# Gate and up of three feed-forwards by Strassen's seven block products, with the modulation sums spread over three engines

## The chip, the core and the metric

The kernel runs on one core of a Trainium2 chip. It uses all five engines: TensorE (PE in the profile) for matrix products, with its weight loads as PEld; VectorE (DVE); ScalarE (ACT); GpSimd (POOL); and SyncE (SP), which issues the DMAs. The metric is the device time of one execution in microseconds.

## The reference

Two layers of a diffusion backbone over 256 latent and 256 context tokens, with a model dimension of 1024. Each layer is a feed-forward, token mixing (attention), and a second feed-forward; each of the three reads a norm that is modulated by vectors computed from the conditioning. All is float32.

```python
def rms_norm(x): return x * rsqrt(mean(x * x, axis=-1) + EPS)
def modulate(h, shift, scale): return h * (1.0 + scale) + shift
def swiglu(h, w_gate, w_up, w_down): return (silu(h @ w_gate) * (h @ w_up)) @ w_down

# layer l: nine vectors of 1024 for the latent tokens (from c), nine for the context tokens (from c_ctx)
m = silu(c) @ w_mod[l] + b_mod[l]            # w_mod[l]: 1024 x 9216
x = x + 0.5 * m[2] * swiglu(modulate(rms_norm(x), m[0], m[1]), ffn1_w_gate[l], ffn1_w_up[l], ffn1_w_down[l])
x = x + m[5] * mix(modulate(rms_norm(x), m[3], m[4]))
x = x + 0.5 * m[8] * swiglu(modulate(rms_norm(x), m[6], m[7]), ffn2_w_gate[l], ffn2_w_up[l], ffn2_w_down[l])
```

The gate and up weights are 1024 x 2816, the down weights 2816 x 1024. The output is the latent stream after two layers, so that the context tokens aren't needed after the second layer's mixing: three feed-forwards have 512 tokens (numbered 1 to 3 below), the last one 256.

## The kernel before

Activations lie transposed: a tile has 128 channels on the partitions and the tokens as columns, the 256 latent tokens first (`HALF[0]`), then the 256 context tokens (`HALF[1]`). Weights are the stationary operand.

**Products in three parts.** A float32 operand is held as a high part (ScalarE copies it to the type that TensorE reads, `fp32r`) and a low part (VectorE subtracts the high part from the operand); `split`, L99, does both. `mm3`, L106, issues three products: high by high, high by low, low by high. `wcols`, L290, loads a block of weights (4 chunks of 128 rows by 256 columns, 512 KB) into a `raw` tile and splits it into an `hs` tile. There are 3 `raw` and 5 `hs` buffers.

**Feed-forward.** `ffn`, L406, goes over 22 chunks of 128 inner columns in pairs, `pair`, L410: gate and up, for each 2 chunks x 8 chunks of the contraction x 3 parts = 48 products of 128 x 128 weights with 512 columns, gathered in PSUM banks `gps` and `ups`; then Silu, product, and a split of the result into an `ah` tile. The 11 pairs come in two parts (`FFN_PARTS`, 6 and 5 pairs). After each part the down products of its chunks (`down`, L477; PSUM `dps`) are added to the stream `xT` by VectorE (`residual`, L313), scaled by the modulation vector. In the last part the second half of the down products is done for each token half apart, so that the next norm can start.

**Modulation.** Except for the first two vectors, the 16 others are sums over the 1024 rows of `w_mod` that run beside the feed-forwards: `mod_load` brings two blocks of 128 x 512, `mod_part`, L198, multiplies each with one scalar a partition and adds it to an accumulator `macc`, once for the latent and once for the context conditioning, all on VectorE. `mod_end`, L209, sums over the partitions with TensorE. `pump_every`, L282, takes one such turn (two blocks) for each 512 columns of products issued, until the list of vectors is done; lists are queued for each feed-forward (six vectors for 1, four for 2, six for 3).

**Order.** The program is written in this order; a scheduler then sets the order of each engine's queue. Queues run in order. SP issues all DMAs.

## Time and profile before

| | us |
|---|---|
| median of 3 executions | 1836.57 |
| lowest, highest | 1834.9, 1838.31 |
| profiled execution, its own time | 1838.31 |
| its span, first to last instruction | 1838.3 |
| TensorE busy in it | 1790.1 |
| VectorE busy | 1278.7 |
| ScalarE busy | 732.8 |
| GpSimd busy | 45.5 |

The times of the profile come from one execution, of the length of the slowest of the three. Busy time is the time in which an engine has an instruction in work; instructions overlap at their edges, so a group's busy time can be less than its count by the mean duration. On TensorE only busy time by count, or the length of a run of products in the chain, tells the pace of products; the mean duration of one holds its way through the array as well. A line in the profile can be that of a helper: L101 is the subtraction in `split`, L104 the product in `mm`, L94 and L97 are `mul` and `add`.

### The profile page before, as it was taken

What the parts mean: (1) busy time and instruction counts of PE and PEld (TensorE: products, weight loads), DVE (VectorE), ACT (ScalarE), POOL (GpSimd) and SP (SyncE); (2) the same over time, 40 slices, a digit from 0 to 9 for tenths busy, and PEclk for the clock granted to TensorE, in tenths of its full rate; (3) what the DMA queues carried; (4) which work ended last, traced back from release to release, by engine and by line L of the source; (5) the groups of instructions that cost most, each with busy time, mean ns of one, the idle gap of its engine ahead of it and who ended that gap; (6) DMA issues with size and microseconds to landing.
All of it is one profiled execution on the core that took longest, in us unless ns stands there. A gap on an engine that the chain in (4) does not pass through costs nothing.

```text
span 1838.3 us, 27533 instructions
## 1 busy us (share of the span) xinstructions
PE 1790.1 (97%) x10851; PEld 1549.1 (84%) x10851; DVE 1278.7 (70%) x2458; ACT 732.8 (40%) x1316; POOL 45.5 (2%) x25
## 2 busy tenths in 40 slices
PE   7999999999999989999999999999999988999999
PEld 4788888898998888888888988888889987789998
DVE  5998776457788699877434667777336787877564
ACT  4323122335666553221223333212234656664442
POOL 0000000011010000000000000000001011000000
PEclk9999999999999989999999999999999999999999
DMA  9856564322110246656323245564333542146552
GB/s 301 271 192 195 191 195 135 117 60 79 49 59 19 65 130 214 207 191 207 116 92 104 77 128 193 186 210 146 91 115 87 101 99 57 47 150 206 172 184 81
DMA packets 229549, 253.80 MB, mean 138 GB/s; under 512 B 21388, under 2 KB 195628, under 8 KB 229420
## 3 DMA queue, kind: packets, MB, share of 16 engines
q1 hardware_dynamic: 229420, 252.05, 44.4%
q8 instruction: 85, 1.39, 0.3%
q14 instruction: 44, 0.36, 0.1%
HBM read 250.96 MB, written 1.05 MB: 137 GB/s over the span
## 4 chain that ended last, share of the span: by engine, by line
PE 85%; DVE 7%; ACT 3%; DMA 2%; issue 1%; SPq 1%; DVEq 0%; ACTq 0%
PE ups L104 23%; PE gps L104 23%; PE dps L104 23%; PE ops L104 3%; PE po L781 2%; PE sc L104 2%; DMA bias<-in_d_rpb_dram 1%; DVE hs L101 1%; PE mps L213 1%; PE paq L104 1%; PE trp L684 1%; PE pbk L104 1%; PE pbv L104 1%; PE bpo L104 1%; PE pak L104 1%
## 5 line engine op out<-in xcount | busy, mean ns | idle before, releaser
L100 ACT ACTIVATE hs<-raw 128x1024 fp32r<-128x1024 f32 (+2 forms) x308 | 315.4, 1030 | 611.9 <-PE dps L104 195.3
L101 DVE TENSOR_TENSOR hs<-raw,hs 128x1024 fp32r<-128x1024 f32 (+2 forms) x308 | 366.9, 1196 | 228.3 <-ACT hs L100 226.2
L104 PE MATMUL dps<-ah,hs 128*128 128x512 f32 (+1 forms) x2256 | 403.5, 338 | 0.2 <-DVE hs L101 0.2
L104 PEld LDWEIGHTS dps<-ah,hs 128*128 128x128 f32 x2256 | 349.8, 190 | 47.7 <-issue 2.5
L104 PE MATMUL gps<-hT,hs 128*128 128x512 f32 (+1 forms) x1680 | 377.8, 381 | 3.8 <-ACT hT L567 2.7
L104 PE MATMUL ups<-hT,hs 128*128 128x512 f32 (+1 forms) x1680 | 374.9, 379 | 0.0
L104 PEld LDWEIGHTS gps<-hT,hs 128*128 128x128 f32 x1680 | 304.1, 190 | 66.0 <-ACT hT L567 3.5
L104 PEld LDWEIGHTS ups<-hT,hs 128*128 128x128 f32 x1680 | 303.2, 189 | 60.3 <-issue 2.4
L206 DVE SCALAR_TENSOR_TENSOR macc<-mraw,const,macc 128x512 f32<-128x512 f32 x448 | 308.7, 745 | 2.7 <-DMA mraw<-in_w_mod_dram 2.5
L320 DVE SCALAR_TENSOR_TENSOR xT<-dps,const,xT 128x256 f32<-128x256 f32 x112 | 50.2, 478 | 78.4 <-PE dps L104 78.3
L100 ACT ACTIVATE ah<-af 128x512 fp32r<-128x512 f32 (+1 forms) x88 | 50.3, 572 | 99.5 <-DVE af L94 68.1
L301 POOL TENSOR_TENSOR hs<-raw,hs 128x1024 fp32r<-128x1024 f32 (+2 forms) x21 | 45.3, 2160 | 1582.8 <-ACT hs L300 1505.9
L104 PE MATMUL gps<-hTl,hs 128*128 128x258 f32 x528 | 66.8, 284 | 1.6 <-DVE hTl L398 1.0
L104 PEld LDWEIGHTS gps<-hTl,hs 128*128 128x128 f32 x528 | 64.7, 190 | 2.5 <-DVE hTl L398 1.2
L104 PE MATMUL ups<-hTl,hs 128*128 128x258 f32 x528 | 65.5, 283 | 0.0
L104 PEld LDWEIGHTS ups<-hTl,hs 128*128 128x128 f32 x528 | 64.4, 190 | 0.0
L101 DVE TENSOR_TENSOR ah<-af,ah 128x512 fp32r<-128x512 f32 (+1 forms) x88 | 54.4, 619 | 13.4 <-ACT ah L100 13.1
L453 ACT ACTIVATE sg<-gps 128x512 f32<-128x512 f32 x66 | 38.3, 588 | 57.9 <-PE gps L104 57.9
L94 DVE TENSOR_TENSOR af<-sg,ups 128x512 f32<-128x512 f32 x66 | 45.1, 685 | 22.5 <-PE ups L104 22.1
L709 DVE TENSOR_REDUCE nm<-sc 128x1 f32<-128x512 f32 (+1 forms) x80 | 53.7, 681 | 5.9 <-PE sc L104 5.8
L715 ACT ACTIVATE pr<-sc,nm 128x512 f32<-128x512 f32 (+1 forms) x64 | 40.3, 635 | 14.9 <-DVE nm L709 14.2
L329 ACT ACTIVATE sq<-xT 128x256 f32<-128x256 f32 (+1 forms) x54 | 23.5, 448 | 51.0 <-DVE xT L320 50.8
(303 smaller groups left out, 1950.0 us busy)
## 6 DMA issues: line engine op xcount, KB each, us to landing
mraw<-in_w_mod_dram SPq DMA_DIRECT2D x128, 512.0 KB, 4.7
raw<-in_ffn_w_gate_dram SPq DMA_DIRECT2D x88, 512.0 KB, 4.1
raw<-in_ffn_w_up_dram SPq DMA_DIRECT2D x88, 512.0 KB, 4.4
raw<-in_ffn_w_down_dram SPq DMA_DIRECT2D x80, 512.0 KB, 3.4
raw<-in_cd_w_in_dram SPq DMA_DIRECT2D x18, 512.0 KB, 4.0
wm<-in_w_mod_dram SPq DMA_DIRECT2D x16, 512.0 KB, 8.6
raw<-in_ab_w_in_dram SPq DMA_DIRECT2D x16, 512.0 KB, 4.1
raw<-in_ffn_w_down_dram SPq DMA_DIRECT2D x16, 256.0 KB, 2.7
```

Source lines behind the costliest of these rows:

```text
L94: V.tensor_tensor(out=out_, in0=a, in1=b, op=ALU.mult)
L100: S.activation(h, src, AF.Copy)
L101: V.tensor_tensor(out=l, in0=src, in1=h.bitcast(F32), op=ALU.subtract)
L104: T.matmul(ps, a, b, start=start, stop=stop)
L206: V.scalar_tensor_tensor(out=acc[:, v], in0=raw[:, i], scalar=c, in1=acc[:, v], op0=ALU.mult, op1=ALU.add)
L301: nc.gpsimd.tensor_tensor(out=hs[:, 1, :n], in0=raw[:, :n], in1=hs[:, 0, :n].bitcast(F32), op=ALU.subtract)
L320: V.scalar_tensor_tensor(out=xT[dc][:, a:e], in0=ps[:, a:e], scalar=modT[:, l, v, m, dc:dc + 1], in1=xT[dc][:, a:e], op0=ALU.mult, op1=ALU ...
L329: S.activation(sq[:, cols], xT[dc][:, cols], AF.Square)
L453: S.activation(sg, g[:, :ntok], AF.Silu)
L709: V.tensor_reduce(out=nm[:, c], in_=view, axis=AX.X, op=ALU.max, negate=True)
L715: S.activation(p[:, cols], sc[:, cols], AF.Exp, bias=nm[:, i + b:i + b + 1], accum_out=den[:, i + b:i + b + 1])
L781: T.matmul(po[64 * x:64 * x + 64, q], val(x, c), pts[x][c], start=c == order[0], stop=c == order[-1], tile_position=(0, 64 * x))
```

## The change

It has two parts.

**Seven products.** In feed-forwards 1 to 3 all pairs but the first (`FFN_PLAIN`) are done by `quad_pair`, which calls `quad` for gate and again for up: 60 quads in all. A quad takes the weights of a pair as 2 x 2 blocks (contraction halves by the two chunks) and the activations as 2 x 2 blocks (contraction halves by token halves), and makes the pair's result from seven block products in place of eight, each 4 chunks x 3 parts = 12 products of 256 columns, by Winograd's form of Strassen's scheme. The combined weight blocks are sums that GpSimd makes of the raw weights (`wquads`: four sums of 128 x 512), and all seven blocks are split. The combined activation blocks are made once a norm, by GpSimd (`combine`: 16 sums of 128 x 256) from unsplit copies that ScalarE keeps (`keep`). VectorE sums the block products out of PSUM (four sums a quad). Parts are now of 3, 3, 3 and 2 pairs, so that each feed-forward has four stages of down products; the last, 256-token feed-forward keeps 6 and 5 pairs and plain products.

**Modulation.** VectorE keeps the latent half. For the context half ScalarE scales the block in place and GpSimd adds it to the accumulator. The context half of four vectors of the second layer, which nothing reads, is left out.

Buffers: `hs` has 8 tiles of half the size (a quad takes seven), `raw` 5, the weights of the first two vectors (`wm`) 6 instead of 16.

```diff
-FFN_PARTS = (6, 5)
+FFN_PARTS = {(0, 1): (3, 3, 3, 2), (0, 2): (3, 3, 3, 2), (1, 1): (3, 3, 3, 2), (1, 2): (6, 5)}
+FFN_PLAIN = {(0, 1): 1, (0, 2): 1, (1, 1): 1, (1, 2): 11}
...
-    def mod_part(acc, raw, k):
+    def mod_part(acc, raw, k, both):
         for i in range(2):
-            for v in range(2):
-                c = cT[:, k + i, v:v + 1]
-                if k + i == 0:
-                    V.tensor_scalar(out=acc[:, v], in0=raw[:, i], scalar1=c, scalar2=None, op0=ALU.mult)
-                else:
-                    V.scalar_tensor_tensor(out=acc[:, v], in0=raw[:, i], scalar=c, in1=acc[:, v], op0=ALU.mult,
-                                           op1=ALU.add)
+            c = cT[:, k + i, 0:1]
+            if k + i == 0:
+                V.tensor_scalar(out=acc[:, 0], in0=raw[:, i], scalar1=c, scalar2=None, op0=ALU.mult)
+            else:
+                V.scalar_tensor_tensor(out=acc[:, 0], in0=raw[:, i], scalar=c, in1=acc[:, 0], op0=ALU.mult,
+                                       op1=ALU.add)
+        for i in range(2 if both else 0):
+            c = cT[:, k + i, 1:2]
+            if k + i == 0:
+                S.activation(acc[:, 1], raw[:, i], AF.Copy, scale=c)
+            else:
+                S.activation(raw[:, i], raw[:, i], AF.Copy, scale=c)
+                nc.gpsimd.tensor_tensor(out=acc[:, 1], in0=raw[:, i], in1=acc[:, 1], op=ALU.add)
...
+    def wquads(w, fp):
+        a = []
+        for b in range(2):
+            raw = rawp.tile([P, 1024], F32, tag="raw", name="rq")
...
+        (a11, a21), (a12, a22) = [[t[:, x] for x in range(2)] for t in a]
+        sw = [unit("sw", "sw") for _ in range(3)]
+        s3, s2, s1 = [t.rearrange("p (k f) -> p k f", f=P) for t in sw]
+        G = nc.gpsimd.tensor_tensor
...
+        parts("a12", a12)
+        parts("a11", a11)
+        G(out=s3, in0=a11, in1=a21, op=ALU.subtract)
+        G(out=s1, in0=a21, in1=a22, op=ALU.add)
+        G(out=s2, in0=s1, in1=a11, op=ALU.subtract)
+        parts("s3", s3)
+        parts("s2", s2)
+        G(out=a21, in0=a12, in1=s2, op=ALU.subtract)
+        parts("s1", s1)
+        parts("s4", a21)
+        parts("a22", a22)
...
+    def combine():
+        G = nc.gpsimd.tensor_tensor
+        for j in range(4):
+            t = hL[j]
+            for i, (a, b) in enumerate(((1, 0), (2, 1), (2, 0), (3, 2))):
+                G(out=t[:, i], in0=t[:, a], in1=t[:, b], op=ALU.subtract)
+            hC[j] = [hp.tile([P, 4, 256], R32, tag="hS", name="hC", bufs=UNITS["hS"]) for _ in range(2)]
+            split(*hC[j], t)
...
+            def prod(ps, x):
+                an, bk = b[x]
+                for k in range(4):
+                    mm3(ps, a[an][:, 0, k], a[an][:, 1, k], bk(k, 0), bk(k, 1), k == 0, k == 3)
...
+            pump_every(512)
+            x, y, z, e = [bank(tag, f"{nm}q{tag}") for tag in ("mm", "sc", "mm", "sc")]
+            prod(x[:, lat], "p2")
+            prod(e[:, lat], "p1")
+            s1 = unit("wq", f"{nm}p1")[:, lat]
+            S.activation(s1, e[:, lat], AF.Copy)
+            prod(x[:, ctx_], "p6")
+            t, r = unit("wq", f"{nm}t"), unit("wq", f"{nm}r")
+            add(two(t), two(x), both(s1))
+            prod(y[:, ctx_], "p7")
+            prod(y[:, lat], "p5")
+            add(two(r), two(y), both(t[:, ctx_]))
+            add(t[:, ctx_], y[:, lat], r[:, ctx_])
+            pump_every(512)
+            prod(z[:, ctx_], "p4")
+            prod(z[:, lat], "p3")
+            add(r, r, z)
+            return t, r
```

What it makes of the queues is shown at three places, all in feed-forward 1. TensorE, one pair in the middle of its last part before (`gps` and `ups` in two banks each):

```order
L104 MATMUL gps_2272<-hT,hs 128x512 x12
L104 MATMUL gps_2273<-hT,hs 128x512 x12
L104 MATMUL gps_2272<-hT,hs 128x512 x12
L104 MATMUL gps_2273<-hT,hs 128x512 x12
L104 MATMUL ups_2284<-hT,hs 128x512 x12
```

TensorE, gate's quad of a pair in the third part after (`hB` and `hT` are norm tiles, `hC` the combined ones, `gqmm` and `gqsc` PSUM banks):

```order
L107 MATMUL gqmm<-hT,hs 128x256 x12
L107 MATMUL gqsc<-hB,hs 128x256 x12
L107 MATMUL gqmm<-hC,hs 128x256 x12
L107 MATMUL gqsc<-hC,hs 128x256 x24
L107 MATMUL gqmm<-hC,hs 128x256 x12
L107 MATMUL gqmm<-hT,hs 128x256 x12
```

48 products of 512 columns have become 84 of 256. VectorE, around the same pair before (`hs<-raw` is a weight block's low part, `af` gate by up, `ah` its low part):

```order
L101 TENSOR_TENSOR hs<-raw,hs 128x1024
L206 SCALAR_TENSOR_TENSOR macc<-mraw,const,macc 128x512 x2
L101 TENSOR_TENSOR hs<-raw,hs 128x1024
L94 TENSOR_TENSOR af<-sg,ups_2284 128x512
L101 TENSOR_TENSOR ah<-af,ah 128x512
L94 TENSOR_TENSOR af<-sg,ups_2285 128x512
```

VectorE, a stretch of the second part after (`rq` and `sw` are raw and combined weight blocks, `gt` and `gr` the sums of products):

```order
L100 TENSOR_TENSOR gt<-gqmm,gp_2016 128x512
L208 SCALAR_TENSOR_TENSOR macc<-mraw,const,macc 128x512
L104 TENSOR_TENSOR hs<-rq,hs 128x512
L208 SCALAR_TENSOR_TENSOR macc<-mraw,const,macc 128x512
L100 TENSOR_TENSOR gr<-gqsc,gt 128x512
L104 TENSOR_TENSOR hs<-sw,hs 128x512
L100 TENSOR_TENSOR gt<-gqsc,gr 128x256
L104 TENSOR_TENSOR hs<-sw,hs 128x512 x2
L100 TENSOR_TENSOR gr<-gr,gqmm 128x512
```

Sums out of PSUM now stand between the low parts of the next quad's weights. GpSimd before, its whole work of the program (low parts of the mixing layers' weights):

```order
L301 TENSOR_TENSOR hs<-raw,hs 128x1024 x6
L301 TENSOR_TENSOR hs<-raw,hs 128x512 x2
L301 TENSOR_TENSOR hs<-raw,hs 128x1024 x7
L301 TENSOR_TENSOR hs<-raw,hs 128x768 x3
L301 TENSOR_TENSOR hs<-raw,hs 128x512 x2
L301 TENSOR_TENSOR hs<-raw,hs 128x1024
```

GpSimd after, two quads of the third part of feed-forward 1 (L344 to L349 are the four sums of `wquads`, L216 the context half of the modulation):

```order
L344 TENSOR_TENSOR sw<-rq 128x512
L216 TENSOR_TENSOR macc<-mraw,macc 128x512 x4
L345 TENSOR_TENSOR sw<-rq 128x512
L346 TENSOR_TENSOR sw<-sw,rq 128x512
L349 TENSOR_TENSOR rq<-rq,sw 128x4x128
L344 TENSOR_TENSOR sw<-rq 128x512
L216 TENSOR_TENSOR macc<-mraw,macc 128x512 x3
L345 TENSOR_TENSOR sw<-rq 128x512
L346 TENSOR_TENSOR sw<-sw,rq 128x512
L349 TENSOR_TENSOR rq<-rq,sw 128x4x128
```

The feed-forwards, in which GpSimd had nothing before, now give it four sums a quad and up to four for the modulation.

## Rows read from the trace of the kernel before

**Rows 1.** The page, parts 1 and 2: span, busy time by engine, granted clock in 40 slices.

```profile
span 1838.3 us, 27533 instructions
PE 1790.1 (97%) x10851; PEld 1549.1 (84%) x10851; DVE 1278.7 (70%) x2458; ACT 732.8 (40%) x1316; POOL 45.5 (2%) x25
...
PEclk9999999999999989999999999999999999999999
```

**Rows 2.** The chain that ended last, in order of time: start, us, what (three pieces).

```profile
58.90 10.88 PE gps L104 x48
...
193.99 38.11 PE dps L104 x168
...
1709.67 34.55 PE dps L104 x288
```

**Rows 3.** Windows, all engines: feed-forward 1 with modulation running, feed-forward 2 after it.

```profile
core 0: us, PE busy (x) PEld busy (x) DVE busy (x) ACT busy (x) POOL busy (x), PEclk, DMA share, GB/s
120.00:160.00 40.00, 40.00 (x190) 32.36 (x189) 33.82 (x54) 11.89 (x16) 0.00 (x0) 1.00 0.53 177
880.00:920.00 40.00, 40.00 (x178) 33.10 (x178) 14.20 (x16) 11.89 (x15) 0.00 (x0) 1.00 0.40 120
```

**Rows 4.** Groups by line and form, VectorE and ScalarE: names, shapes, count | busy us, mean ns | idle.

```profile
L101 DVE TENSOR_TENSOR hs<-raw,hs 128x1024 fp32r<-128x1024 f32 x286 | 348.4, 1224 | 227.5 <-ACT hs L100 225.5 <-DMA bias<-in_d_rpb_dram 1.5
...
L206 DVE SCALAR_TENSOR_TENSOR macc<-mraw,const,macc 128x512 f32<-128x512 f32 x448 | 308.7, 745 | 2.7 <-DMA mraw<-in_w_mod_dram 2.5
...
L320 DVE SCALAR_TENSOR_TENSOR xT<-dps,const,xT 128x256 f32<-128x256 f32 x112 | 50.2, 478 | 78.4 <-PE dps L104 78.3
...
L101 DVE TENSOR_TENSOR ah<-af,ah 128x512 fp32r<-128x512 f32 x66 | 45.2, 687 | 13.4 <-ACT ah L100 13.1
...
L94 DVE TENSOR_TENSOR af<-sg,ups 128x512 f32<-128x512 f32 x66 | 45.1, 685 | 22.5 <-PE ups L104 22.1
...
L100 ACT ACTIVATE ah<-af 128x512 fp32r<-128x512 f32 x66 | 41.2, 625 | 68.1 <-DVE af L94 68.1
...
L453 ACT ACTIVATE sg<-gps 128x512 f32<-128x512 f32 x66 | 38.3, 588 | 57.9 <-PE gps L104 57.9
```

**Rows 5.** The page, part 6: issue of the first norm's modulation weights, count, KB, us to landing.

```profile
wm<-in_w_mod_dram SPq DMA_DIRECT2D x16, 512.0 KB, 8.6
```

**Rows 6.** Timeline from 376.3 us, GpSimd and VectorE: start us, us, engine, line, operation.

```profile
start us, us, engine line op out<-in xcount [idle before <-releaser]
...
376.56 2.41 POOL L301 TENSOR_TENSOR hs<-raw,hs 128x1024 fp32r<-128x1024 f32 x1 [376.12 <-ACT hs L300]
376.78 0.88 DVE L320 SCALAR_TENSOR_TENSOR xT<-dps,const,xT 128x256 f32<-128x256 f32 x2 [4.48 <-PE dps L104]
...
378.14 0.48 DVE L320 SCALAR_TENSOR_TENSOR xT<-dps,const,xT 128x256 f32<-128x256 f32 x1 [0.48 <-PE dps L104]
...
378.54 0.97 DVE L97 TENSOR_TENSOR const<-const,sq 128x512 f32<-128x512 f32 x1
```

**Rows 7.** Timeline from 1626 us, GpSimd and VectorE.

```profile
1626.10 2.40 POOL L301 TENSOR_TENSOR hs<-raw,hs 128x1024 fp32r<-128x1024 f32 x1 [39.03 <-PE ops L104]
...
1626.51 2.54 DVE L101 TENSOR_TENSOR hs<-raw,hs 128x512 fp32r<-128x512 f32 x1
```

**Rows 8.** Timeline from 1406.3 us, VectorE and GpSimd.

```profile
1406.33 1.21 DVE L101 TENSOR_TENSOR hs<-raw,hs 128x1024 fp32r<-128x1024 f32 x1
...
1406.97 2.84 POOL L301 TENSOR_TENSOR hs<-raw,hs 128x1024 fp32r<-128x1024 f32 x1 [8.16 <-ACT hs L300]
```

**Rows 9.** Groups by line and form, GpSimd.

```profile
L301 POOL TENSOR_TENSOR hs<-raw,hs 128x1024 fp32r<-128x1024 f32 x14 | 34.6, 2473 | 1444.2 <-ACT hs L300 1367.3 <-PE ops L104 39.0 <-DMA bias<-in_d_rpb_dram 27.9
L301 POOL TENSOR_TENSOR hs<-raw,hs 128x768 fp32r<-128x768 f32 x3 | 5.5, 1869 | 10.7 <-ACT hs L300 10.7
L301 POOL TENSOR_TENSOR hs<-raw,hs 128x512 fp32r<-128x512 f32 x4 | 5.1, 1287 | 127.9 <-ACT hs L300 127.9
```

**Rows 10.** Windows, all engines, around a drop of the granted clock (columns as above).

```profile
640.00:655.00 15.00, 12.20 (x102) 12.00 (x100) 14.52 (x35) 9.47 (x20) 0.00 (x0) 1.00 0.13 36
655.20:665.40 10.20, 7.35 (x31) 6.87 (x32) 9.75 (x27) 4.44 (x12) 0.00 (x0) 0.50 0.61 206
```

**Rows 11.** Windows, TensorE products into gps alone: busy (count), clock, DMA share, GB/s.

```profile
661.20:665.40 4.20, 4.20 (x19) 0.50 0.45 172
```

More of the change, by code (lines that the diff above doesn't have):

```diff
@@ L1 @@
 import math
-from contextlib import ExitStack
+from contextlib import ExitStack, nullcontext
 import concourse.bass as bass
@@ L293, in wcols @@
         raw = rawp.tile([P, 1024], F32, tag="raw", name="raw")
-        Q.dma_start(out=raw[:, :n].rearrange("p (k f) -> p k f", k=nk), in_=src)
+        last_load[0] = Q.dma_start(out=raw[:, :n].rearrange("p (k f) -> p k f", k=nk), in_=src).ins
         if tag is None:
-            hs = hsp.tile([P, 2, 1024], R32, tag="hs", name="hs")
+            parts = [hsp.tile([P, 1024], R32, tag="hs", name="hs")[:, :n] for _ in range(2)]
         else:
-            hs = big("hw", tag)
+            hw = big("hw", tag)
+            parts = [hw[:, s, :n] for s in range(2)]
@@ L310, in tile_hybrid_dit, with hx, new_hT @@
     hT = [None] * KC
+    def hx(k, s, sl):
+        t = hT[k]
+        if isinstance(t, tuple):
+            v = sl.start // 256
+            return t[v][:, s, sl.start - 256 * v:sl.stop - 256 * v]
+        return t[:, s, sl]
+    def new_hT(split_):
+        two = [[hp.tile([P, 2, 2, 256], R32, tag="hB", name="hB", bufs=UNITS["hB"]) for _ in range(2)]
+               for _ in range(2)] if split_ else []
+        for k in range(KC):
+            if split_ and k < 4:
+                hT[k] = tuple(t[k // 2][:, k % 2] for t in two)
+            else:
+                hT[k] = hp.tile([P, 2, NTOK], R32, tag="hT", name="hT")
     summed = set()
@@ L364, in norm_half @@
         if v == 0:
-            for k in range(KC):
-                hT[k] = hp.tile([P, 2, NTOK], R32, tag="hT", name="hT")
+            new_hT(m != 3)
         bc = norm_stats(l, m, v)
@@ new lines, in quad_pair @@
+        def quad_pair(g):
+            with tc.issue_after(last_load[0]) if g == FFN_PLAIN[l, n] else nullcontext():
+                gs = quad("g", wg, g)
+                for t in gs:
+                    S.activation(t, t, AF.Silu)
+                us = quad("u", wu, g)
+            ah = [big("ah") for _ in range(2)]
+            for i, (sg, t) in enumerate(zip(gs, us)):
+                mul(t, t, sg)
+                for s in range(2):
+                    flat = ah[s].rearrange("p i n -> p (i n)")
+                    o = flat[:, 256:768] if i else bass.AP(tensor=flat.tensor, offset=flat.offset, ap=[flat.ap[0], [768, 2], [1, 256]])
+                    if s == 0:
+                        S.activation(o, t if i else t.rearrange("p (x n) -> p x n", x=2), AF.Copy)
+                        hi = o
+                    else:
+                        V.tensor_tensor(out=o, in0=t if i else t.rearrange("p (x n) -> p x n", x=2), in1=hi.bitcast(F32), op=ALU.subtract)
+            return [[ah[s][:, i] for s in range(2)] for i in range(2)]
@@ L468, in ffn @@
         f0 = 0
-        for part, npair in enumerate(FFN_PARTS):
+        n = 1 if m_gate == 2 else 2
+        for part, npair in enumerate(FFN_PARTS[l, n]):
             acts = []
             for fp in range(npair):
-                acts += pair(f0 // 2 + fp, 2 * fp, part == 0 and fp == 0)
+                if f0 // 2 + fp < FFN_PLAIN[l, n]:
+                    acts += [[t[:, s] for s in range(2)]
+                             for t in pair(f0 // 2 + fp, 2 * fp, part == 0 and fp == 0)]
+                else:
+                    acts += quad_pair(f0 // 2 + fp)
@@ L473, in ffn @@
             nf = 2 * npair
-            last = part == 1
-            if mixing is not None and not last:
+            last = part == len(FFN_PARTS[l, n]) - 1
+            if mixing is not None and part == 0:
                 next(mixing)
@@ L587, in tile_hybrid_dit @@
         V.tensor_copy(bcs[:, HALF[v]], norm_bcast(rs0[:, 2 * v:2 * v + 2])[:, :256])
-    hT[:] = [hp.tile([P, 2, NTOK], R32, tag="hT", name="hT") for k in range(KC)]
+    new_hT(True)
     first_mods(0, wm0)
```

98 lines of the change are left out of this document (69 added, 29 removed).

## The prediction

> **What bounds the kernel now.** I began with the page's busy shares. The matrix engine (PE) is busy 1790.1 of 1838.3 us, so 48 us are left in which it isn't; VectorE (DVE) stands at 70%, GpSimd (POOL) at 2% [rows 1]. The chain of waits then shows what a feed-forward is made of: runs of nothing but products. 48 of them with 512 columns take 10.88 us (227 ns each), 168 take 38.11 us; 288 with 256 columns take 34.55 us (120 ns each) [rows 2]. A product of half the width thus costs 53%, not 50%. Inside a feed-forward the windows show PE busy 40.00 of 40 us, with DVE at 33.82 while the modulation stream runs and at 14.20 once it is done [rows 3]. So PE sets the time, and every product that goes is worth its 120 or 227 ns, as long as the other engines keep delivering weights. DVE has 6 us in 40 to spare in the first kind of stretch. That is the number to watch, since the change puts work on DVE's side in all of them.
>
> The execution profiled took 1838.31 us, its span 1838.3; the median of the three is 1836.57, 1.7 us less. A difference of 0.2% (4 us) is about what a measurement of this kernel can tell from no change.
>
> **What the change saves on PE.** A chunk pair's gate (or up) was 48 products of 512 columns, 10.88 us [rows 2]. As a "quad" it is 7 block products of 12, 84 products of 256 columns: 84 x 0.120 = 10.08 us. Each of the 60 quads saves 0.80 us, 48 us in all. Smaller shares of the down products come in halves (288 + 528 half-width ones instead of 1248: about -3 us) and half of the first pair of feed-forward 1 becomes half-width (+1 us). PE: -50 us.
>
> The Trainium skill (TensorE: Matmul & The Clock Gate, Back-to-back issue gap) gives the spacing of single products as columns / 2.4 + 2.5 ns, 109 ns at 256 and 216 ns at 512. By that a quad would save 1.2 us and the change 72 us; the rows say 120 and 227 ns, and they decide.
>
> **What it puts on the other engines.** For each quad, by the code and the order:
> - Splits of seven 512-column blocks into high and low parts instead of two of 1024: ACT seven copies, DVE seven subtractions of two SBUF tiles.
> - GpSimd four sums of 512 columns on the weights, 240 in all, plus 16 sums of 256 columns at each of three norms.
> - DVE four sums that read PSUM (2.4 us by the 0.69 us of a 512-column sum [rows 4] and half for the short one).
> - For a pair, DVE's products of gate and up and the low parts of the result, as before, but now all from SBUF: 2 a quad.
> - The modulation stream: DVE keeps the latent half (256 of 512 operations); the context half becomes a scaling on ACT and a sum on GpSimd (168), and is dropped for four of the 16 vectors.
>
> ACT carries this: 7 x 0.63 + half of two Silu and two copies, 1.2, + 0.4 + at most 2.2 for modulation = 8.2 us a quad, under 10.1 [rows 4]. The loads keep their number and size. Early loads have 6 buffers instead of 16: 0 to 8.6 us (one round of them [rows 5]); I take 3, as most of the first pair's products stand before the last quarter. The 96 more residual updates (48 for each of two more parts, 0.45 us [rows 4]) read PSUM and lie in the down stages, where DVE has room.
>
> **What decides: GpSimd and DVE exclude each other.** At 376.56 a GpSimd sum runs for 2.41 us. Three DVE updates that read PSUM pass beside it at their usual 0.48 us. Then a 512-column sum of two SBUF tiles starts at 378.54 and ends at 379.51, 0.54 us after GpSimd's end at 378.97 [rows 6]. At 1626.51 a weight split of 512 columns takes 2.54 us instead of 0.69 and ends 0.55 us after GpSimd [rows 4, 7]. The other way round too: at 1406.97 GpSimd finds DVE in a split, takes 2.84 instead of 2.41 us, and ends 2.27 us after that split [rows 8]. So of a GpSimd sum and a DVE operation with two SBUF inputs only one runs at a time, for its whole length, and their times add up. Before, GpSimd worked 45.5 us in the whole program [rows 1]; now it has 408 sums of 512 columns inside the feed-forwards, and nearly all of DVE's work there has two SBUF inputs: splits, modulation, the result's products and low parts.
>
> Prices. A DVE operation of 512 columns: 0.69 us alone, 0.55 behind a GpSimd sum; I take 0.62 (the two will alternate, but not always). Of 1024: 1.22 and, by the same 0.14 less, 1.09; I take 1.15. GpSimd's of 512: 1.29 alone [rows 9], 1.15 with the 0.14 us that the row at 1406.97 hides; I take 1.20. Of 256, an estimate from 1.29, 1.87 and 2.47 us for 512, 768 and 1024 [rows 9]: 0.65.
>
> One quad with both halves of the modulation: 13 DVE operations x 0.62 + 7.5 GpSimd sums x 1.20 = 17.1 us, against PE's 10.1. With the latent half alone: 13 x 0.62 + 4 x 1.20 = 12.9. Without modulation: 9 x 0.62 + 4.8 = 10.4. The sums that read PSUM (2.4) I take as hidden under GpSimd's time. Since PE needs the splits of each quad, and the buffers hold little more than one quad's seven blocks, it can't run ahead.
>
> Now the sum over the stretches. Each feed-forward has four blocks of products (a plain pair and 4 quads; 6; 6; 4 quads), each followed by its down products (33 us, the last 24). I counted the operations of each block in the order. The second block of feed-forward 1: DVE 36 splits, 27 modulation steps, 12 products and low parts, 2 short weight splits, 77 x 0.62 = 48, and 3 x 1.15; GpSimd 24 + 22 sums x 1.20 = 55. Together 106 us, against 60.5 of PE: +46. The others in the same way, as operations on DVE (of 512, of 1024) and GpSimd, excess over PE:
> - Feed-forward 1: first block 60, 9 and 24 (+16 short), 94 against 62, of which 10 lie in the start-up: +22. Second: +46. Third 70, 3 and 48: 104 against 60.5, +44. Fourth, no modulation, 31, 4 and 16: +3. In all +115.
> - Feed-forward 2: 67, 8 and 28 (+16 short), 5 us of it before the first product: +31. 78, 3 and 49: +50. 50, 3 and 31: +11. Fourth +2. In all +94.
> - Feed-forward 3 (latent half alone for four of six vectors): 66, 9 and 34 (+16 short), 8 us before the first product: +35. 76, 3 and 24: +19. 61, 3 and 24: +10. Fourth +2. In all +66.
>
> The down stages come out about even: in the first of feed-forward 1, DVE's 18 us and GpSimd's 17 sums, 20 us, against 33; the others have less, and I leave these 5 us to the range.
>
> Sum: 1838 - 50 + 275 + 3 = 2066, against the median 2064; I say **2065 us**, 12% slower. At the low prices (0.55, 1.09, 1.15) the 944 us of such work shrink by 8%: 1990. At the high ones (0.69, 1.22, 1.29): 2150. With none of the 2.4 us hidden in the 48 quads of the first three blocks, 115 more: 2265.
>
> **Rivals.**
> - *Faster after all.* GpSimd's sums fall into the time that DVE spends on PSUM (2.4 us a quad, and the residual updates) or waits for ACT and PE, and exclusion costs little. DVE alone then needs 13 x 0.62 + 2.4 = 10.5 us a quad, PE 10.1: about even, and the 50 us are gained: 1790. The point is where the two engines' sum passes PE's 10.1 us a quad; by the rows it is passed by 7 us while modulation runs for both halves. For it: 408 sums are only 490 us, beside some 1040 us of products (60 x 10.08, three pairs of 21.8 and three times 123 of down products). Against: DVE's two-input work there is 620 us more. 10%.
> - *The clock falls as well.* PE waits inside most quads. At 655.2 its granted clock shows 0.50 (1.2 of 2.4 GHz) for 10.2 us, after 15 us in which it was busy 12.20 [rows 10]; there 19 half-width products took 4.20 us [rows 11], 221 ns each, a quad 18.6 us. If it stayed there through the first three blocks of all three (136 us more a feed-forward than PE's full speed), the time would be 1838 - 50 + 408 = 2196. For it: PE would be busy 60% of such a block. Against: at half speed it waits no longer, and comes back. 15%. The Trainium skill (TensorE: Matmul & The Clock Gate, HAM oscillation — how this bites in real kernels) describes just this, bursts that each start at half rate behind a wait for data; the row at 655.2 agrees with it for one wait, and no row here shows it over a long stretch.
> - *Late sums.* DVE's queue is in order. A sum that reads PSUM stands between splits, and while it waits for a product the next quad's splits wait behind it, GpSimd's buffers with them. That is the 2265 above. 5%.
>
> **How the numbers follow.** The forecast itself has 68%, within no change 2%, the rivals 10, 15 and 5%. The range of 1930 to 2200 takes in both ends of the prices and the clock's case; left out are the gain, no change and the time above 2200. Faster 0.10, same 0.02, slower 0.88.
>
> **What would show it.** Right: GpSimd busy about 550 us; DVE's splits of 512 columns at well over 0.69 us on average, those beside a GpSimd sum ending 0.55 us behind it; PE's waits for DVE's splits the longest of all; blocks with both modulation halves near 17 us a quad, those at the end near 10.5. The clock's part: stretches at 0.5 in the first three blocks. Wrong: PE still above 95% busy in the feed-forwards, GpSimd's sums beside two-input DVE work without stretching it, or ACT late instead.

## The result, and the profile after

The changed kernel takes 2082.74 us (median of 4 executions, 2080.02 to 2084.0) against 1836.9 before (4 executions in the same session): a ratio of 1.1335, with a 95% interval of 1.1319 to 1.1351. The forecast was 2065, with a range of 1930 to 2200. It is 246 us slower.

The page of the kernel after, parts 1 and 2, beside [rows 1]:

```profile
span 2082.1 us, 33783 instructions
...
PE 1838.2 (88%) x12811; PEld 1672.8 (80%) x12811; DVE 1716.5 (82%) x2858; ACT 1022.6 (49%) x1940; POOL 748.7 (36%) x481
...
PEclk9898998999999988888999989999999999999999
```

GpSimd has gone from 45.5 to 748.7 us, VectorE from 1278.7 to 1716.5. PE's share fell from 97% to 88%, and its clock is no longer full in the feed-forwards. The groups by line and form show what VectorE's and GpSimd's operations now last (busy, mean ns, then idle time before them); [rows 4] and [rows 9] have the same operations before: 745 ns for a modulation step, 687 for a split of 512 columns, 1287 for a GpSimd sum:

```profile
L208 DVE SCALAR_TENSOR_TENSOR macc<-mraw,const,macc 128x512 f32<-128x512 f32 x224 | 239.1, 1068 | 24.7 <-DMA mraw<-in_w_mod_dram 23.3
L104 DVE TENSOR_TENSOR hs<-rq,hs 128x512 fp32r<-128x512 f32 x240 | 230.2, 974 | 22.5 <-ACT hs L103 22.3
L104 DVE TENSOR_TENSOR hs<-sw,hs 128x512 fp32r<-128x512 f32 x180 | 208.7, 1184 | 12.7 <-ACT hs L103 12.3
...
L216 POOL TENSOR_TENSOR macc<-mraw,macc 128x512 f32<-128x512 f32 x168 | 265.6, 1582 | 233.9 <-ACT mraw L215 181.7 <-issue 46.2 <-DVE nrm L460 1.5
L345 POOL TENSOR_TENSOR sw<-rq 128x512 f32<-128x512 f32 x60 | 97.5, 1625 | 162.5 <-DMA rq<-in_ffn_w_gate_dram 82.6 <-DMA rq<-in_ffn_w_up_dram 52.3 <-PE gqsc L107 9.0
```

The idle time ahead of VectorE's groups is short, but their operations last up to 1.7 times as long as alone. Sorted by what GpSimd did meanwhile, splits of `rq` that meet no GpSimd operation last 682 ns on average (135 of them), those that meet a sum of 512 columns 1354 (101). A record of busy time here holds waiting that no semaphore shows. The timeline of the kernel after, from 349.9 us, VectorE and GpSimd, in the third block of feed-forward 1:

```profile
349.94 1.59 POOL L346 TENSOR_TENSOR sw<-sw,rq 128x512 f32<-128x512 f32 x1
350.34 1.75 DVE L208 SCALAR_TENSOR_TENSOR macc<-mraw,const,macc 128x512 f32<-128x512 f32 x1
351.61 1.60 POOL L349 TENSOR_TENSOR rq<-rq,sw 128x512 f32<-128x512 f32 x1
352.01 1.75 DVE L104 TENSOR_TENSOR hs<-sw,hs 128x512 fp32r<-128x512 f32 x1
...
353.17 1.71 POOL L344 TENSOR_TENSOR sw<-rq 128x512 f32<-128x512 f32 x1
353.68 0.68 DVE L100 TENSOR_TENSOR ur<-uqsc,ut 128x512 f32<-128x512 f32 x1
354.28 1.15 DVE L208 SCALAR_TENSOR_TENSOR macc<-mraw,const,macc 128x512 f32<-128x512 f32 x1
```

Read the ends. GpSimd ends at 351.53, VectorE's modulation step at 352.09, 0.56 us behind; GpSimd's next at 353.21, 1.12 behind that; VectorE's split at 353.76, 0.55 behind. They take turns, 1.67 us for a pair, though each record shows 1.6 to 1.75 us for one. The sum that reads PSUM (353.68) passes beside GpSimd in 0.68 us. The Trainium skill (SBUF — State Buffer, SBUF: two separate sides) says that the two engines share a pair of SBUF ports as an exclusive lock: of a VectorE operation with two SBUF inputs and a GpSimd operation that reads SBUF, the one that starts first holds it for the whole instruction, and the other waits. The turns in these rows agree.

Windows of the kernel after, all engines (columns as in [rows 3]): in feed-forward 1 the first down stage, the second and third blocks of products, and the fourth, which has no modulation left:

```profile
135.90:185.40 49.50, 39.86 (x165) 30.33 (x163) 48.02 (x70) 19.83 (x31) 37.35 (x23) 0.86 0.47 150
185.40:271.20 85.80, 71.02 (x525) 67.48 (x524) 84.36 (x100) 46.83 (x81) 55.31 (x36) 0.92 0.44 135
...
314.60:412.00 97.40, 73.83 (x541) 69.98 (x540) 95.25 (x107) 48.23 (x83) 65.29 (x41) 0.89 0.45 134
...
444.80:485.00 40.20, 40.20 (x337) 40.20 (x336) 33.68 (x47) 22.01 (x36) 11.36 (x7) 1.00 0.45 132
```

VectorE is busy for 97 to 98% of the first three, PE for 76 to 83%; in the last, four quads take 40.20 us with PE busy throughout, 10.05 each. PE stands idle for 244 us of the span, before for 48. Of its waits (us in all, times, longest), those for the low parts of quads are the longest in total; three lines of the list:

```profile
PE gqmm L107 <- DVE hs L104: 29.0, 15, 4.4
PE nst L107 <- DVE const L100: 19.7, 5, 7.0
PE mps L227 <- POOL macc L216: 14.2, 7, 3.9
```

By stages, from the first product of one to the first of the next: feed-forward 1 takes 489 us instead of 385, 2 takes 452 instead of 372, 3 takes 412 instead of 374, and the mixing layers 266 and 240 instead of 253 and 229.

### The profile page after: what moved, and what is told of

It is laid out like the page before. It is cut to its first block, busy times and chain, and to the rows that moved or that the text cites. A ratio compares the mean times of both kernels' runs of the same rounds, so it can differ in the third digit from the quotient of the medians.

```text
span 2082.1 us, 33783 instructions
## 1 busy us (share of the span) xinstructions
PE 1838.2 (88%) x12811; PEld 1672.8 (80%) x12811; DVE 1716.5 (82%) x2858; ACT 1022.6 (49%) x1940; POOL 748.7 (36%) x481
## 4 chain that ended last, share of the span: by engine, by line
PE 27%; DVE 15%; issue 4%; DMA 3%; ACT 2%; POOL 1%; SPq 0%; DVEq 0%; ACTq 0%; POOLq 0%
PE dps L107 9%; DVE hs L104 5%; PE ups L107 3%; PE gps L107 3%; DMA mraw<-in_w_mod_dram 2%; DVE macc L208 2%; PE uqmm L107 2%; PE gqmm L107 2%; PE uqsc L107 1%; DVE xT L387 1%; PE gqsc L107 1%; DVE const L100 1%; DMA bias<-in_d_rpb_dram 1%; PE po L941 1%; POOL hL L407 1%
## 5 line engine op out<-in xcount | busy, mean ns | idle before, releaser
L216 POOL TENSOR_TENSOR macc<-mraw,macc 128x512 f32<-128x512 f32 x168 | 265.6, 1582 | 233.9 <-ACT mraw L215 181.7
L104 DVE TENSOR_TENSOR hs<-raw,hs 128x1024 fp32r<-128x1024 f32 (+3 forms) x212 | 253.0, 1201 | 56.3 <-ACT hs L103 52.1
L208 DVE SCALAR_TENSOR_TENSOR macc<-mraw,const,macc 128x512 f32<-128x512 f32 x224 | 239.1, 1068 | 24.7 <-DMA mraw<-in_w_mod_dram 23.3
L103 ACT ACTIVATE hs<-raw 128x1024 fp32r<-128x1024 f32 (+3 forms) x212 | 196.4, 941 | 109.4 <-PE dps L107 67.1
L104 DVE TENSOR_TENSOR hs<-rq,hs 128x512 fp32r<-128x512 f32 x240 | 230.2, 974 | 22.5 <-ACT hs L103 22.3
L215 ACT ACTIVATE mraw<-mraw,const 128x512 f32<-128x512 f32 x168 | 120.5, 720 | 211.6 <-DVE macc L208 180.8
L104 DVE TENSOR_TENSOR hs<-sw,hs 128x512 fp32r<-128x512 f32 x180 | 208.7, 1184 | 12.7 <-ACT hs L103 12.3
L103 ACT ACTIVATE hs<-rq 128x512 fp32r<-128x512 f32 x240 | 143.8, 620 | 76.3 <-PE dps L107 33.2
L344 POOL TENSOR_TENSOR sw<-rq 128x512 f32<-128x512 f32 x60 | 102.8, 1713 | 156.5 <-DMA rq<-in_ffn_w_gate_dram 150.0
L345 POOL TENSOR_TENSOR sw<-rq 128x512 f32<-128x512 f32 x60 | 97.5, 1625 | 162.5 <-DMA rq<-in_ffn_w_gate_dram 82.6
L107 PE MATMUL gqmm<-hC,hs 128*128 128x256 f32 x720 | 109.0, 301 | 35.6 <-DVE hs L104 25.5
L103 ACT ACTIVATE hs<-sw 128x512 fp32r<-128x512 f32 x180 | 105.4, 621 | 46.4 <-PE dps L107 23.1
L107 PE MATMUL gqmm<-hT,hs 128*128 128x256 f32 x720 | 105.5, 299 | 13.2 <-DVE ut L100 6.3
```

The source lines that it names most:

```text
L103: S.activation(h, src, AF.Copy)
L104: V.tensor_tensor(out=l, in0=src, in1=h.bitcast(F32), op=ALU.subtract)
L107: T.matmul(ps, a, b, start=start, stop=stop)
L208: V.scalar_tensor_tensor(out=acc[:, 0], in0=raw[:, i], scalar=c, in1=acc[:, 0], op0=ALU.mult, op1=ALU.add)
L215: S.activation(raw[:, i], raw[:, i], AF.Copy, scale=c)
L216: nc.gpsimd.tensor_tensor(out=acc[:, 1], in0=raw[:, i], in1=acc[:, 1], op=ALU.add)
```

## Experiments

All times are device times; the kernel before took 1835 to 1838 us beside each group. Where one number is given, it is that of one execution.

### GpSimd's sums: what they cost, and by what

**One column of the context sums.** ScalarE's scaling, the steps and their order stay; the other 511 columns of these 168 sums are left out.

```diff
-                nc.gpsimd.tensor_tensor(out=acc[:, 1], in0=raw[:, i], in1=acc[:, 1], op=ALU.add)
+                nc.gpsimd.tensor_tensor(out=acc[:, 1, 0:1], in0=raw[:, i, 0:1], in1=acc[:, 1, 0:1], op=ALU.add)
```

> The changed kernel with GpSimd's 168 sums of the context modulation cut to one column (the context modulation vectors are then wrong; DVE's and ScalarE's work is unchanged). Exclusion theory (a GpSimd sum and a DVE operation with two SBUF inputs never run together): a quad with both modulation halves falls from 17.1 to about 13 us, the whole by about 140 us to 1945 us, and DVE's modulation steps and weight splits get shorter on average. DVE-overload theory (DVE has too many operations by itself): no change, 2083 us.

Measured: 1959.78, 123 us less than after. VectorE's modulation steps fell from 1068 to 875 ns, its splits of `rq` from 974 to 843, though nothing of VectorE's own work was taken away:

```profile
L104 DVE TENSOR_TENSOR hs<-rq,hs 128x512 fp32r<-128x512 f32 x240 | 198.2, 843 | 27.4 <-ACT hs L103 27.1
L208 DVE SCALAR_TENSOR_TENSOR macc<-mraw,const,macc 128x512 f32<-128x512 f32 x224 | 195.9, 875 | 24.7 <-DMA mraw<-in_w_mod_dram 23.2
```

**GpSimd busy, but reading nothing.** In place of each context sum, two fills of the same tile.

```diff
-                nc.gpsimd.tensor_tensor(out=acc[:, 1], in0=raw[:, i], in1=acc[:, 1], op=ALU.add)
+                for _ in range(2):
+                    nc.gpsimd.memset(acc[:, 1], 0.0)
```

> The changed kernel with each of GpSimd's 168 context sums replaced by two GpSimd fills of the same 512 columns, which write SBUF but read nothing (the context modulation is left out). Exclusion theory, if it is reading that excludes: like the narrow sums, about 1945 us, although GpSimd's queue is held for longer by each. Late-GpSimd theory (what costs is that GpSimd's own queue is too slow for its work): stays above 2040 us as long as two fills take about as long as a sum did.

Measured: 1951.61. Groups of that kernel:

```profile
L217 POOL MEMSET macc<- 128x512 f32 x336 | 179.4, 534 | 190.3 <-ACT macc L213 164.8 <-DVE macc L208 8.3 <-DMA rq<-in_ffn_w_up_dram 1.8
...
L208 DVE SCALAR_TENSOR_TENSOR macc<-mraw,const,macc 128x512 f32<-128x512 f32 x224 | 207.3, 926 | 13.7 <-DMA mraw<-in_w_mod_dram 11.9
L104 DVE TENSOR_TENSOR hs<-rq,hs 128x512 fp32r<-128x512 f32 x240 | 198.7, 844 | 27.4 <-ACT hs L103 27.2
```

336 fills keep GpSimd busy for 179 us, and VectorE's splits of `rq` stay at 844 ns, as with the narrow sums. The modulation steps are at 926 ns against 875, but not by the fills: steps that meet fills alone last 743 ns (59 of them), steps that meet no GpSimd operation 744 (96), and steps that meet one of the weight sums, which stay in this kernel, 1451 (40). So it isn't a busy GpSimd or its late queue that costs, but its reading.

**Neither context sums nor weight sums.** The context sums narrow, and the four sums of weights a quad as well, each followed by a fill of its tile:

```diff
...
+        def G1(out, in0, in1, op):
+            G(out=out[:, 0, 0:1], in0=in0[:, 0, 0:1], in1=in1[:, 0, 0:1], op=op)
+            nc.gpsimd.memset(out, 0.02)
...
```

> The changed kernel with the context sums (as in e1_narrow) and the sums of weights one column wide on GpSimd, the latter followed by a fill; both are so left out of the computation. DVE keeps the latent half of the modulation. e1_narrow took 1960. Theory (exclusion is nearly all of the loss): DVE by itself then sets the quads that carry modulation, 13 x 0.69 + 2.4 = 11.4 us against 10.07, for about 45 quads 60 us over g2_bare's forecast of 1812: 1875 (1850 to 1900). Rival (DVE's queue order): 1940 or more, since e1_narrow has already lost the longer sums.

Measured: 1858.69 (1855.17 to 1862.17), ratio 1.0115, interval 1.0099 to 1.013. The weight sums cost another 101 us. Groups of it:

```profile
L208 DVE SCALAR_TENSOR_TENSOR macc<-mraw,const,macc 128x512 f32<-128x512 f32 x224 | 171.0, 764 | 30.9 <-DMA mraw<-in_w_mod_dram 29.6
L104 DVE TENSOR_TENSOR hs<-rq,hs 128x512 fp32r<-128x512 f32 x240 | 162.3, 692 | 37.8 <-ACT hs L103 37.0
L104 DVE TENSOR_TENSOR hs<-sw,hs 128x512 fp32r<-128x512 f32 x180 | 120.1, 687 | 36.8 <-ACT hs L103 35.2 <-POOL sw L345 1.1 <-POOL sw L346 0.2
```

These operations of VectorE are within 3% of the durations that they have alone. So 224 of the 246 us hang on GpSimd's reading sums, and 22 on everything else. A narrow weight sum with its fill also takes GpSimd about 0.9 us instead of the 1.29 of a full sum alone; how much of the 101 us comes from weights that are ready sooner, no run separates.

### Who else could take the work, and does the clock bind

**The context half back on VectorE**, as before the change, with the quads unchanged:

```diff
...
-                S.activation(raw[:, i], raw[:, i], AF.Copy, scale=c)
-                nc.gpsimd.tensor_tensor(out=acc[:, 1], in0=raw[:, i], in1=acc[:, 1], op=ALU.add)
+                V.scalar_tensor_tensor(out=acc[:, 1], in0=raw[:, i], scalar=c, in1=acc[:, 1], op0=ALU.mult,
+                                       op1=ALU.add)
```

> The changed kernel with the context half of the modulation back on DVE, GpSimd left with the weights' sums alone. Exclusion theory: 17 DVE operations x 0.62 + 4 GpSimd sums x 1.20 = 15.3 us a quad instead of 17.1, about 45 us less in all, 2035 us. DVE-overload theory: slower, 2145 us. Late-GpSimd theory: near 1850 us.

Measured: 2050.06, 33 us under the changed kernel. By the turns above, a sum on GpSimd costs VectorE 1.12 us, and the same step on VectorE itself 0.55 to 0.75: GpSimd is the dearer place. ScalarE's scaling goes with the sums here, so the 33 us are for both.

**Two of three products a quad**, which takes 28 of a quad's 84 products off PE:

```diff
-                    mm3(ps, a[an][:, 0, k], a[an][:, 1, k], bk(k, 0), bk(k, 1), k == 0, k == 3)
+                    mm(ps, a[an][:, 0, k], bk(k, 0), k == 0, False)
+                    mm(ps, a[an][:, 1, k], bk(k, 0), False, k == 3)
```

> The changed kernel with two of three products in each quad (weights' parts by the activations' high part alone; a third of the quads' products is left out). Exclusion theory: the blocks with modulation keep their length since PE is not what they wait for, only the quads without modulation can shrink to GpSimd's and DVE's 10 us; 2040 to 2080 us. Clock theory (the time was lost because PE ran at half clock): a third of PE's time in the quads goes, 60 x 28 x 0.12 = 200 us, to about 1880 us.

Measured: 2050.03. PE lost a third of the quads' products and the kernel 33 us; the fourth blocks, which have no modulation, account for 27 of these (40.3 to 30.8 us in feed-forward 1, 40.0 to 31.4 and 40.3 to 31.6 in the others). The mean granted clock fell to 0.899, which at the two levels of 1.0 and 0.5 is (1 - 0.899) x 2 x 2048 = 414 us at half, against (1 - 0.943) x 2 x 2082 = 237 in the changed kernel and 37 before, and yet it is no slower. PE stands idle for 335 us of this kernel against 244 in the changed one: in the blocks with modulation its own pace isn't what they wait for.

### Each part alone

**Modulation alone**: the kernel before with the new `mod_part` and `mod_end`, and plain pairs.

> The kernel before with the change's modulation alone (context half scaled on ScalarE and summed on GpSimd, the four unread context halves left out), all pairs plain. Exclusion theory: a plain pair with both halves has on DVE 4 low parts of 1024 columns x 1.15, 8 modulation steps and 2 low parts x 0.62, 10.8 us, and 7 GpSimd sums x 1.20, 8.4 us, together 19.2 us against PE's 21.8: hidden, so within 0.5% of the kernel before, 1830 to 1845 us. Late-GpSimd theory: slower, since the same 168 sums stand in GpSimd's queue.

Measured: 1858.62 (1858.31 to 1860.28), ratio 1.0118, interval 1.0103 to 1.0133. The expectation missed: 21 us are lost, 11 of them in the first block of feed-forward 1 (158.7 us, before 147.7) and 8 in that of feed-forward 2. Timeline of that kernel, from 108.5 us:

```profile
108.49 6.84 POOL L213 TENSOR_TENSOR macc<-mraw,macc 128x512 f32<-128x512 f32 x4 [2.68 <-ACT mraw L212]
109.39 2.59 DVE L205 SCALAR_TENSOR_TENSOR macc<-mraw,const,macc 128x512 f32<-128x512 f32 x2 [1.04 <-DMA mraw<-in_w_mod_dram]
...
111.90 0.41 DVE L227 COPY mst<-mps 128x256 f32<-128x256 f32 x1
...
112.36 0.69 PE L231 MATMUL mpt<-const,mst 128*128 128x128 f32 x2 [9.29 <-DVE mst L227]
```

The transposes at the end of a modulation vector (`mpt`) stand in PE's queue and wait 9.29 us for VectorE's copy. What the copy reads was there at 97.4, but it stands behind steps of the next vector: these wait for a block of weights (VectorE idle for 4.34 us up to 101.52) whose buffer GpSimd's sum gave back only at 98.32, and are stretched besides. The gate's products, which need nothing of this, wait behind the transposes, and from 105.4, within the wait, the granted clock is at half for 10.2 us. The second block of feed-forward 1 stays at 112.0 us beside 21 of GpSimd's sums, with VectorE busy 65 us of it: where VectorE has room, they cost nothing.

**Quads without modulation sums**: all but the first of each vector are one column wide, on both engines; the rest of the sums is left out. Loads and ScalarE's scaling stay.

> The changed kernel with all modulation sums beyond each first block cut to one column on GpSimd and on DVE (the modulation vectors are wrong; loads and ScalarE's scaling stay): the seven products by themselves. Prediction's sum: 1837 - 50 + 3 = 1790 us. Cover theory (the last part, now of two pairs, leaves a shorter stretch of down products to hide the next norm behind, 5.8 us a token half where it was 14.4, and the mixing layers start late): 10 to 25 us more, 1800 to 1815 us.

Measured: 1921.4. Missed by over 100 us: the quads and their 240 weight sums lose 84 us by themselves. VectorE is busy 60 to 63 us of 69 in such blocks, so there is room on average; what is late is single operations. Timeline of that kernel in feed-forward 3, from 1233.6 us:

```profile
1233.64 1.50 POOL L345 TENSOR_TENSOR sw<-rq 128x512 f32<-128x512 f32 x1 [4.24 <-DMA rq<-in_ffn_w_gate_dram]
1233.97 0.37 ACT L587 ACTIVATE gp<-gqsc 128x256 f32<-128x256 f32 x1
...
1235.22 1.60 POOL L346 TENSOR_TENSOR sw<-sw,rq 128x512 f32<-128x512 f32 x1
1235.61 1.75 DVE L617 TENSOR_TENSOR ah<-ur,ah 128x512 fp32r<-128x512 f32 x1
...
1236.89 1.59 POOL L349 TENSOR_TENSOR rq<-rq,sw 128x512 f32<-128x512 f32 x1
1237.29 1.74 DVE L104 TENSOR_TENSOR hs<-sw,hs 128x512 fp32r<-128x512 f32 x1
...
1238.95 0.68 DVE L100 TENSOR_TENSOR gt<-gqmm,gp 128x512 f32<-128x512 f32 x1
...
1239.78 0.55 PE L107 MATMUL gqmm<-hC,hs 128*128 128x256 f32 x1 [5.56 <-DVE gt L100]
```

`gt`, the first sum of gate's products, could have been made from 1234.3. It stands behind an `ah` and an `hs` operation that each wait out a whole GpSimd sum, so it starts at 1238.95, and PE, which needs its bank, stands for 5.56 us; from 1237.3, within this wait, its clock is at half for 6.8 us. The rival of late sums is at work here, but as a consequence of the exclusion.

**Quads meant to be kept away from modulation**: both halves on VectorE, 7, 3 and 3 of 11 pairs plain, no turn of modulation issued inside quads (in the program; the down stages of feed-forward 3 issue 1.75 times as many); and the same in parts of 3, 4 and 4 pairs.

```diff
-FFN_PLAIN = {(0, 1): 1, (0, 2): 1, (1, 1): 1, (1, 2): 11}
+FFN_PLAIN = {(0, 1): 7, (0, 2): 3, (1, 1): 3, (1, 2): 11}
...
```

> Modulation and seven products apart: DVE does both modulation halves again (the unread ones left out), and plain pairs stand where modulation runs (7, 3 and 3 of 11), quads after it, without any modulation step inside a quad; in the second layer's first feed-forward the down stages take 1.75 times as many. Exclusion theory: 40 quads at PE's pace gain 40 x 0.8 = 32 us, half-width products in the plain pairs cost 8: 1810 us; with the shorter cover of the last part (cover theory) up to 1834 us.

> The same with parts of 3, 4 and 4 pairs in place of 3, 3, 3 and 2: the last part's down products of one token half take 11.5 us instead of 5.8 and cover more of the next norm. Cover theory: 10 to 20 us less than the version with a last part of two pairs. Without it: the same time.

Measured: 1927.61 (ratio 1.0498, interval 1.048 to 1.0515) and 1928.21 (1.0497, 1.0481 to 1.0513). Both missed: still 90 us slower than before, and the longer last part changed nothing in the sum. The edit doesn't do what it was meant to: in the queues as they came out, 103 of VectorE's 392 modulation steps start while quads run (76 in the second kernel). In the two blocks of 4 quads without any, a quad takes 10.1 us; in the blocks of 6 with 9 to 22 of them, 10.9 to 11.8. So these two runs don't part quads from modulation. Besides, I had charged all of the loss to quads beside modulation; the next group shows the rest.

### The bare quads, and what they need beside them

**No long sum at all**: `e5_no_mods` with the weight sums narrowed as in `g1_no_gps`.

> The kernel of e5_no_mods (every modulation sum one column wide, on both engines) in which also each of GpSimd's four sums of weights per quad is one column wide, followed by a fill of the whole tile with a constant; so the weights' sums are left out of the computation, and GpSimd reads nothing of any length inside the feed-forwards. e5_no_mods took 1921. Theory (what is left there is still the exclusion between GpSimd's 240 sums and DVE's work: DVE's sums that read PSUM come late behind stretched splits, and PE waits for them): the quads run at PE's pace of 10.07 us, as the blocks of four without modulation did, and the time is 1838 - 50 + 24 (what the two mixing layers have been longer in every variant) = 1812, with a few us of clock 1805 to 1830. Rival (the order of DVE's queue alone, with the PSUM banks, holds PE up, whatever GpSimd does): hardly under e5_no_mods, 1890 to 1920.

Measured: 1842.03 (1839.4 to 1843.39), ratio 1.0024, interval 1.0015 to 1.0034. 79 us under the quads with their weight sums, so PE's late banks hung on GpSimd's sums, and the order of VectorE's queue alone is refuted. But with every sum free, the quads only come level with the kernel before: 12 us above the theory's end.

**The parts alone**: the kernel before in parts of 3, 3, 3 and 2, in all four feed-forwards.

```diff
-FFN_PARTS = (6, 5)
+FFN_PARTS = (3, 3, 3, 2)
...
-            last = part == 1
-            if mixing is not None and not last:
+            last = part == 3
+            if mixing is not None and part == 0:
```

> The kernel before with one edit: its feed-forwards in four parts of 3, 3, 3 and 2 chunk pairs instead of two of 6 and 5, no quads and the modulation as it was. Theory (the 13 and 11 us that both mixing layers lost in every variant come from the short last part, whose down products give little cover to the next norm): the mixing layers are longer by 10 or more each and the time is 1855 to 1865. Rival (they come from what the quads need beside them: buffers, the sums for the norm, the split states): the mixing layers stay at 253 and 229, and the time within 8 us of 1837, as 96 more residual updates read PSUM and lie in stages in which DVE has room.

Measured: 1857.66 (1857.12 to 1857.71), ratio 1.0108, interval 1.0093 to 1.0123. The total is the theory's, the place is not: the mixing layers are 3 and 2 us longer, and 13 us lie in feed-forwards 2 and 3 (759 us together, before 746). 6.98 of these are one wait of PE for the norm, in the first block of feed-forward 3, which follows the short last part of feed-forward 2; there is no such wait before. A down stage takes 34.2 us; the first of feed-forward 1:

```profile
101.90:136.10 34.20, 34.20 (x165) 27.58 (x163) 33.64 (x71) 9.67 (x12) 0.00 (x0) 1.00 0.71 240
```

Windows of `g2_bare` and then of this kernel over the first mixing layer:

```profile
402.70:666.10 263.40, 243.56 (x1823) 222.55 (x1821) 205.48 (x526) 157.57 (x385) 19.37 (x18) 0.96 0.17 53
```

```profile
408.10:664.40 256.30, 240.56 (x1824) 220.34 (x1824) 202.08 (x524) 156.60 (x384) 12.57 (x6) 0.98 0.17 51
```

So against the same parts the quads gain 31 us in the feed-forwards (1113.4 us for the three against 1144.6) and give back 7 and 10 in the mixing layers. In PE's busy time they save 35 us (1755.8 against 1790.4). Why the mixing layers are longer stays open: PE idles 20 us instead of 16 there and its clock is lower, and it isn't the modulation sums, the weight sums (both are one column wide in `g2_bare`) or the parts (5 us in `g3_parts`).

**Quads in the last part alone** (12 quads; both halves on VectorE; nothing left out). No modulation step starts beside these quads:

```diff
-FFN_PLAIN = {(0, 1): 1, (0, 2): 1, (1, 1): 1, (1, 2): 11}
+FFN_PLAIN = {(0, 1): 9, (0, 2): 9, (1, 1): 9, (1, 2): 11}
...
```

> The changed kernel with quads for the last two chunk pairs of each of the three feed-forwards alone (12 quads, in the fourth part, where no modulation runs), plain pairs elsewhere, and both halves of the modulation on DVE as before; nothing is left out. Theory (such quads run at PE's pace, 40.3 us for four against 43.5, and what the kernel needs beside them costs the same as in the other runs: the parts 20, the two mixing layers 22 together as in g2_bare): 1837 + 20 + 22 - 10 = 1869, and 1865 to 1885 with the first block's half-width pair (8 us longer in g2_bare than in g3_parts). Rival (the mixing layers are longer because of the quads' work that runs into them, not because of what is kept for them): with 12 quads only, 1837 + 20 - 10 = 1847, up to 1855.

Measured: 1895.26 (1893.32 to 1896.55), ratio 1.0314, interval 1.0296 to 1.0331. The quads gain what was forecast (40.0 to 40.3 us for four, 43.5 in `g3_parts`), and the mixing layers are 5 and 13 us longer than in `g3_parts` with 12 quads, 7 and 10 with 60, so that rival falls; but the total is 10 over the range's end. What was not forecast lies in the plain pairs. Three of them, with little modulation left (12 and 9 operations of it), in this kernel and in `g3_parts`:

```profile
895.40:963.00 67.60, 67.60 (x433) 61.58 (x432) 29.91 (x37) 18.46 (x23) 0.00 (x0) 1.00 0.34 109
```

```profile
870.90:936.20 65.30, 65.30 (x290) 54.06 (x289) 27.51 (x34) 17.74 (x23) 0.00 (x0) 1.00 0.43 137
```

PE is busy throughout in both. The quads need half of the norm's chunks in two token halves; a plain pair beside quads therefore does half of its products at half width and takes 0.77 us longer, 27 of them by that 21 us. That eats the gain of the quads, 0.8 us each, wherever plain pairs stay. No run here is faster than the kernel before.

## Why the prediction was right, and where its steps were not

- **What bounds.** Right. VectorE's room was 6 us in 40 [rows 3], and the change spent it. Quads with both halves were to take near 17 us each; the second and third block of feed-forward 1 took 14.3 and 16.2.
- **PE, -50.** A quad takes 10.05 us, 10.08 was forecast. By the Trainium skill's spacing of single products (TensorE: Matmul & The Clock Gate, Back-to-back issue gap), 109 ns at 256 columns, a block of four quads would take 36.7 us as an estimate; 40.20 was measured. In PE's busy time 35 of the 50 us show (`g2_bare` against `g3_parts`). In `g2_bare` the clock is at half for 26 us more ((1 - 0.983) x 2 x 1840 = 63 against 37). PE is busy in 54 us of that time there and in 28 in `g3_parts`, which costs it 13 us more of full pace: most of the gap.
- **The exclusion.** Right in kind, and it decided: 224 us by subtraction (2083 to 1960 to 1859). The pair was priced at 0.62 + 1.20 = 1.82 us; the turns take 0.55 + 1.12 = 1.67. I took the middle of the rows where the low end held, so this term of the sum was too large: 275 us forecast for the stretches, 224 measured by subtraction.
- **The sum by feed-forwards** came out nearly as forecast: with PE's saving of 17 each, +98, +77 and +49 were due, 224; +104, +79 and +38 came, 222. That is in part luck. At the prices stated, the operations listed for the three first blocks come to 87, 95 and 102 us, not to the 94, 98 and 105 that their excesses take: the sum should have been 13 us lower, about 2052. And inside, the time lay elsewhere. The second blocks were forecast at +46, +50 and +19 over PE's 60.5 us and came at +25, +29 and +9; the third at +44, +11 and +10, and came at +37, +5 and +11. "The down stages come out about even" is the step that failed: the first ones are 15, 14 and 5 us longer than the 34.2 of `g3_parts`, the second 9, 7 and 5. For the first of feed-forward 1 I had counted 18 us of VectorE and 17 sums; 23 sums of GpSimd ran there, 14 of them for the context, and VectorE was busy 48.02 of 49.50 us, against 33.64 of 34.20 in `g3_parts` without GpSimd. With the context sums narrow (`e1_narrow`) the stage takes 38.6 us: the exclusion was at work in the down stages too.
- **Fourth blocks** (+3, +2, +2): 40.0 to 40.3 us, no excess: what I priced at 10.4 us a quad against PE's 10.1 is hidden under PE there, with only 7 of the 16 weight sums inside the window of feed-forward 1. That doesn't hold wherever the long modulation sums are gone: in `e5_no_mods` the second and third blocks took 60.7 to 76.0 us, not 60.5.
- **What was left out.** The parts: I costed the updates (hidden) and not the norm behind a short last part, 20 us in `g3_parts` in all. The mixing layers: +13 and +11, of which the parts have 3 and 2. The first block: 87.7 us in `g2_bare` against 79.3, where I had 3 for the buffers and 1 for the half-width pair. The first block and most of the parts lie within the feed-forwards' sums, and the exclusion that came cheaper than priced covers them: the total is better than its terms, and that is luck. The mixing layers' 24 us are on top, and are about the 18 us by which the forecast fell short.
- **GpSimd busy about 550.** 748.7: its records are longer than alone too (1582 ns for a context sum, 1287 alone), as VectorE's are.
- **Rivals.** Faster after all: refuted, as GpSimd's sums cost 224 us, and even with no long sum at all (`g2_bare`) the time is 1842 and not 1790. The clock: it did fall, 237 us at half against 37, and PE was busy in 191 us of it; but `e6_two`, with 414 us at half, is no slower, so that this is not what sets the time of the blocks with modulation. The Trainium skill (TensorE: Matmul & The Clock Gate, HAM oscillation — how this bites in real kernels) describes bursts that each start at half rate behind a wait for data; the trace agrees, with 46 stretches of 3.4 to 13.7 us at 0.50, each with a wait of PE ahead of it. Late sums: seen in places (a wait of 5.56 us in `e5_no_mods`), and the 79 us between `e5_no_mods` and `g2_bare` go with GpSimd's sums.
- **Rather than by prices**, the 246 us divide so, taken away in this order: context sums 123, weight sums 101, VectorE's latent half beside the quads 17 (1859 to 1842), and 5 for parts, buffers and mixing layers less the quads' gain.

## What to carry to other kernels

Before work goes to GpSimd, look at what VectorE does at that moment: if both read two tiles from SBUF, the work costs VectorE nearly GpSimd's whole length (1.12 us for a sum of 512 columns here, 1.29 alone), and was cheaper on VectorE itself. Where VectorE had room, it cost nothing (`e4_mods_only`, second block). Price a scheme that saves products together with what its operands must look like (halved tiles, shorter parts, fewer buffers); here that alone ate the gain. An in-order queue turns a stretched operation into a late one: find the short operation behind it for which PE waits.
